# A decoder layer whose gate/up products use seven block products on two more k tiles: eight of ten groups instead of six, with sums, a row norm and transposes at other places

## The chip, the cores and the metric

The kernel runs on one core of a Trainium2 chip. The metric is the device time of one execution in microseconds; the median of several runs is compared. The engines are named as in the profile: PE is the matrix engine and PEld its weight loads, DVE the vector engine, ACT the scalar engine, POOL the general engine, SP the engine that here only issues transfers.

## The reference

One decoder layer on 256 tokens with model width 2048, all in float32: a half-step SwiGLU network of width 5632, a token mixer, and a second SwiGLU network, each followed by a layer norm.

```
def _swiglu(x, w_gate, w_up, w_down):
    return (jax.nn.silu(x @ w_gate) * (x @ w_up)) @ w_down

h = _layer_norm(ALPHA * h + 0.5 * _swiglu(h, ffn1...), ln1_g, ln1_b)
mix = _mixer(h, ...)      # latent attention of 8 heads beside differential attention of 4 heads
h = _layer_norm(ALPHA * h + mix, ln2_g, ln2_b)
h = _layer_norm(ALPHA * h + 0.5 * _swiglu(h, ffn2...), ln3_g, ln3_b)
```

In the mixer one projection gives c_q, c_kv, a rotary key, the differential branch's queries, keys and values, and two gates. The rows of c_q and c_kv pass an RMS norm before the projections to heads. Each differential head's output rows (width 256) pass an RMS norm with gain `subg`; both branches are projected, gated by sigmoids, added and projected again.

## The kernel before

**Precision.** Each float32 weight block of 128 x 1024 (two k tiles of 512 columns) is split into a high and a low part: `split` (L154, L155) casts on ACT to a rounded format, and DVE subtracts to get the low part. A product is then three matmuls of 512 columns (`triple`, L208 to L210): high by high, high by low, low by high. The second of them, L209, is the first that reads the low part of the weights.

**The queue.** All products go through one software queue in program order. `unit(load, prep, now)` issues a unit's loads at once; `prep` (sums and split) runs when more than three units are loaded and `now` (the matmuls) when more than four are prepared. The split parts lie in a ring of six pairs (`wring`). Each `now` is one tick, and `later(n, f)` runs `f` n ticks on. A scheduler may then move instructions of an engine against each other by small distances, unless `issue_after` orders them; `behind_split(n)` puts an instruction behind the low part of the n-th last split.

**Gate/up groups.** Each of the two networks has 11 groups p=0 to 10 of two 512-column weight chunks, each chunk half gate and half up. p=0 is done plainly; p=1 to 10 run in `Hybrid.group`. There the 256 tokens and the two chunks make a 2 x 2 block product, done with seven products (forms 1, 5, 6, 7, 2, 4, 3) instead of eight for k tiles 0 to 7: each form has two weight tiles, s=0 and s=1, of two k tiles each. The remaining k tiles are done plainly, one unit of two k tiles for one chunk (letters `p` and `q` in the order strings). A *wide* group takes k tiles 8 and 9 by the same forms too: a third weight tile s=2 of 128 x 512 columns, in buffers `eraw`, with its token side in `Extra`. A group that is not wide is called *narrow* here. The weight sides of forms 5, 6 and 4 are sums of two blocks, added in place on DVE (L426) ahead of the split; the sum for form 7 comes by an accumulating transfer that POOL issues (L428).

```
order = "15pp6p72q4q3q"        # wide
order = "15pp6p7p2q4q3qq"      # narrow, from p=2 on
hy.group(..., p % 3 != 1, p > 1)   # wide for p = 2, 3, 5, 6, 8, 9
```

The results go by `sum_done` (sums with an earlier copy, L882) to `half` (the product with silu of the gate, L866) and, transposed by `turn_out` (L712), to DRAM. The rows come back as `hraw`, and 13 and 16 ticks after p=10 begins to be queued `split_h` splits two of these row blocks for the down projection (`h`), among the splits of p=9 and p=10. The mixer's two gates use `Hybrid` too, with `small=True`.

**Mixer.** `c_norm(b, i)` computes the RMS norm of a half's c_q or c_kv rows (its last step, the product with the gain, is L1125) and two ticks later transposes them by `turn_out`. `ckv2_done` calls it for c_kv as soon as the last columns are there. `diff_head(h)` has four steps, scores, `turn` (transposes of the probabilities, L1100), `values` (with the norm of the output rows `orow`, L1258) and `turn2` (transposes of these, L1265, and their split `od`); step i of head h runs 2 + 6h + 3i ticks on, beside the products of a gate group.

Of the kernel before, what the change touches and what calls it, by code (L numbers as in the profile page):

```python
# [15 lines left out]
ALU = mybir.AluOpType  # L16
# [7 lines left out]
KF = DFF // P  # L24
# [35 lines left out]
def layer_kernel(ctx: ExitStack, tc: tile.TileContext, a: dict, out: bass.AP):  # L60
    nc = tc.nc
    V, S, GP, PE = nc.vector, nc.scalar, nc.gpsimd, nc.tensor
# [4 lines left out]
    small = ctx.enter_context(tc.tile_pool(name="small", bufs=1))  # L67
# [35 lines left out]
    def later(n, fn):  # L103
        uid[0] += 1
        heapq.heappush(todo, (step[0] + n, uid[0], fn))
# [47 lines left out]
    def split(hi, lo, src):  # L153
        cast[0] = S.copy(hi, src)  # L154
        lows[0] = V.tensor_tensor(out=lo, in0=src, in1=hi.bitcast(F32), op=ALU.subtract)  # L155
        return lows[0]
# [37 lines left out]
    def unit(load, prep, now, later_on=None):  # L194
        if load is not None:
            load()
        loaded.append((prep, now, later_on))
        advance(*ahead)

    def next_pair():  # L200
        assert len(ring) > len(prepared) + lag[0], (len(ring), len(prepared), lag[0])
        catch_up(len(ring) - 1)
        pair = ring.pop(0)
        ring.append(pair)
        return pair

    def triple(o, xh, xl, wh, wl, first, last, again=False):
        PE.matmul(o, xh, wh, start=first, stop=False, skip_group_check=again)  # L208
        PE.matmul(o, xh, wl, start=False, stop=False, skip_group_check=again)  # L209
        PE.matmul(o, xl, wh, start=False, stop=last, skip_group_check=again)  # L210
# [133 lines left out]
    def behind_split(n):  # L344
        return tc.issue_after(line[-n].ins) if len(line) >= n else nullcontext()

    def split_in_line(strict, *a):
        with behind_split(1) if strict else nullcontext():
            line.append(split(*a))

    class Hybrid:
# [22 lines left out]
        def group(self, w0, w1, done, wide=False, seeded=False, gates=False):  # L374
            banks = {}
            small = self.small
            n2, n3, q5, n1 = [t[:, i, :] for t in self.snaps for i in range(2)]
            R = self.raws
# [12 lines left out]
            def bank(n):  # L391
                first = n not in banks
                if first:
                    banks[n] = mm_bank()
                return banks[n], first
# [7 lines left out]
            end_s = 2 if wide else 1  # L403

            def source(name, s):
                w, j0 = blocks[name]
                if s < 2:
                    return w[j0 + s]
                i = j0 // 2
                return w[4][:, i * 512:(i + 1) * 512]  # L410

            def seventh(p, s):
                load_block, src, add, b = plan[p]
                st = {}
                tiles = G if s < 2 else 1

                def load():
                    if s < 2 and load_block in there:
                        return
                    nc.sync.dma_start(R[load_block][s], source(load_block, s))  # L420

                def prep():
                    t = R[src][s]
                    if add is not None and (small or p != 7):
                        with nullcontext() if small else behind_split(s + 1):
                            V.tensor_tensor(out=t, in0=t, in1=R[add[1]][s], op=ALU.add)  # L426
                    if not small and p == 6:
                        nc.gpsimd.dma_start(R["12"][s], source("22", s), accum_op=ALU.add)  # L428
                    pair = [v[:, :tiles * 512] for v in next_pair()]
                    split_in_line(not small, *pair, t)  # L430
                    st["pair"] = [v.rearrange("p (g n) -> p g n", g=tiles) for v in pair]

                def now():
                    o, first = bank(b)
                    wh, wl = st["pair"]
                    for g in range(tiles):
                        if s < 2:
                            xh, xl = (v[:, 2 * s + g, :] for v in self.seven.at_[p])
                        else:
                            xh, xl = self.extra.at_[p]  # L440
                        triple(o, xh, xl, wh[:, g, :], wl[:, g, :], first and g == 0,
                               s == end_s and g == tiles - 1 and p in stops, b in "XZ" or seeded)
                    if s == end_s and p in after:
                        after[p]()
                unit(load if load_block else None, prep, now)
# [403 lines left out]
    def ffn(n, x, wgu, wdn, residual, g, bt, each, first=None, between=None, nxt=None, cols=None, norm=None, pending=None):  # L849
# [78 lines left out]
        for p in range(1, KF // 4):  # L928
            if p == KF // 4 - 1:
                for i, q in enumerate((3, 4, 0)):  # L930
                    later(3 + 3 * i, lambda q=q: get_h(q))
                later(13, lambda: split_h(3))
                later(16, lambda: split_h(4))
            hy.group(wgu[2 * p], wgu[2 * p + 1],
                     lambda n, b, bank, snap, op, p=p: sum_done(2 * p + n, b, bank, snap, op),
                     p % 3 != 1, p > 1)
        ln = LayerNorm(0.5, residual, g, bt, each, nxt, cols,
                       ((24, 26, 48, 50) if pending is None else (13, 14, 60, 62), (94, 97, 100, 103)),
                       35 if cols is None else None, pending, () if pending is None else (17, 32, 67, 82))
# [10 lines left out]
        for p in range(2):  # L950
# [30 lines left out]
            else:  # L981
                call(len(units) - 8, widen)
            down.run(wdn[2 * p], wdn[2 * p + 1], units, forms,
                     lambda m, b, bank, sign, p=p: ln.fold(2 * p + m, b, bank, sign),
                     lambda m, b, bank, p=p: ln.evac(2 * p + m, b, bank), calls, 8 * p)
# [119 lines left out]
    def mixer(x):  # L1105
# [11 lines left out]
        def c_norm(b, i):  # L1117
            c = c_row[b][:, i * RANK:(i + 1) * RANK]
            junk = tmp_tile([P, RANK], "junk")
            ss = sm(1, "ss")  # L1120
            S.activation(junk, c, AF.Square, accum_out=ss)
            ms = sm(1, "ms")
            V.tensor_scalar(out=ms, in0=ss, scalar1=1.0 / RANK, scalar2=None, op0=ALU.mult)
            r = rstd(ms, RMS_EPS, 1)
            V.scalar_tensor_tensor(out=c, in0=c, scalar=r, in1=gain[:, i * RANK:(i + 1) * RANK],  # L1125
                                   op0=ALU.mult, op1=ALU.mult)
            turns[i, b] = dram.tile([P, 512], F32, name=nm("turn"))
            later(2, lambda: turn_out(c, turns[i, b]))
# [7 lines left out]

        def ckv2_done(b, bank):
            S.copy(c_row[b][:, 768:1024], bank[:, 0:256])
            c_norm(b, 1)
            kr = kr_row[b]  # L1140
            V.memset(kr, 0.0)
            rope(kr[:, 0:32].unsqueeze(1), kr[:, 64:96].unsqueeze(1), bank[:, 256:320], b, 1)
            V.tensor_copy(kr[:, 160:256].rearrange("p (a c) -> p a c", a=3)[:, 0:3:2],
                          kr[:, 0:96].rearrange("p (a c) -> p a c", a=3)[:, 0:3:2])
            later(7, lambda: to_cols(kr, krT, b, 2))
# [124 lines left out]

        for h in range(DH):
            for i, f in enumerate(diff_head(h)):
                later(2 + 6 * h + 3 * i, f)
        gate(1, 2, c_back)
        qT = [cols_proj(a["wuq"][c], cn, 4, "qT") for c in range(2)]
        qrT = act_tile([P, 4, T], F32, "qrT")
# [217 lines left out]
```

## Time and profile before

| | |
|---|---|
| median of 3 runs | 1975.17 us (1974.82 to 1975.22) |
| profiled execution | 1975.91 us |
| span of the profiled execution | 1973.9 us, 25650 instructions |
| clock granted to PE | 0.998 of full |
| PE / PEld busy | 1959.4 / 1622.2 us |
| DVE / ACT / POOL busy | 1759.6 / 1260.5 / 287.3 us |
| bytes moved | 484.64 MB, mean 246 GB/s |

The span is what the trace covers; the execution's time has 2.0 us around it. A timeline row gives start, duration, engine, source line, operation, output and inputs; in brackets stands how long the engine was idle before it and who ended that. A row of waits gives the engine and what it waited for, the total in us, how often, and the longest. In the groups by line, the numbers after the bar are busy us, mean ns of one, and idle us before. A matmul is pipelined, so its duration is longer than the step from one to the next.

### The profile page before, as it was taken

What the parts mean: (1) busy time and instruction counts of PE and PEld (TensorE: products, weight loads), DVE (VectorE), ACT (ScalarE), POOL (GpSimd) and SP (SyncE); (2) the same over time, 40 slices, a digit from 0 to 9 for tenths busy, and PEclk for the clock granted to TensorE, in tenths of its full rate; (3) what the DMA queues carried; (4) which work ended last, traced back from release to release, by engine and by line L of the source; (5) the groups of instructions that cost most, each with busy time, mean ns of one, the idle gap of its engine ahead of it and who ended that gap; (6) DMA issues with size and microseconds to landing.
All of it is one profiled execution on the core that took longest, in us unless ns stands there. A gap on an engine that the chain in (4) does not pass through costs nothing.

```text
span 1973.9 us, 25650 instructions
## 1 busy us (share of the span) xinstructions
PE 1959.4 (99%) x8796; PEld 1622.2 (82%) x8796; DVE 1759.6 (89%) x2143; ACT 1260.5 (64%) x1630; POOL 287.3 (15%) x499
## 2 busy tenths in 40 slices
PE   9999999999999999999999999999999999999997
PEld 8888878888888898888887888888888888888886
DVE  8899999999898879988977677789999999999986
ACT  6666666766656566666667765556676766665661
POOL 0112211122100011002223120001212111210000
PEclk9999999999999999999999999999999999999999
DMA  8978888778776667667667668578888877786763
GB/s 318 284 219 270 276 265 249 223 221 297 279 231 227 210 218 257 236 223 259 223 203 243 232 210 275 199 261 256 247 283 279 248 239 237 238 323 234 274 232 123
DMA packets 145747, 484.64 MB, mean 246 GB/s; under 512 B 20768, under 2 KB 20816, under 8 KB 145616
## 3 DMA queue, kind: packets, MB, share of 16 engines
q1 hardware_dynamic: 116208, 397.99, 57.8%
q0 software_dynamic: 29408, 85.02, 16.2%
q8 instruction: 69, 1.13, 0.2%
q14 instruction: 62, 0.51, 0.1%
HBM read 454.08 MB, written 28.84 MB: 245 GB/s over the span
## 4 chain that ended last, share of the span: by engine, by line
PE 94%; DVE 2%; DMA 1%; ACT 1%; issue 1%; SPq 0%; POOL 0%; DVEq 0%; ACTq 0%; POOLq 0%
PE mm L209 30%; PE mm L210 30%; PE mm L208 30%; PE tr L210 1%; PE tr L209 1%; PE tr L208 1%; DVE wring L155 1%; ACT wring L154 1%; PE tr L668 0%; DMA sraw<-in_wgm_dram 0%; DVE sraw L426 0%; DMA sraw<-in_gu_dram 0%; DMA turn<-blocks 0%; PE tr L1298 0%; PE tr L1300 0%
## 5 line engine op out<-in xcount | busy, mean ns | idle before, releaser
L154 ACT CAST wring<-raw 128x1024 fp32r<-128x1024 f32 (+2 forms) x475 | 491.0, 1037 | 319.0 <-PE mm L210 229.9
L155 DVE TENSOR_TENSOR wring<-raw,wring 128x1024 fp32r<-128x1024 f32 (+2 forms) x475 | 566.5, 1200 | 101.4 <-ACT wring L154 99.5
L154 ACT CAST wring<-sraw 128x1024 fp32r<-128x1024 f32 x436 | 452.6, 1052 | 220.0 <-DVE sraw L426 99.9
L155 DVE TENSOR_TENSOR wring<-sraw,wring 128x1024 fp32r<-128x1024 f32 x436 | 520.9, 1217 | 29.3 <-ACT wring L154 25.5
L209 PE MATMUL mm<-wring,h 128*128 128x512 f32 (+2 forms) x1260 | 485.1, 385 | 0.1
L210 PE MATMUL mm<-wring,h 128*128 128x512 f32 (+2 forms) x1260 | 485.2, 385 | 0.0
L208 PE MATMUL mm<-wring,h 128*128 128x512 f32 (+2 forms) x1260 | 484.8, 385 | 0.0
L209 PE MATMUL mm<-wring,xs 128*128 128x512 f32 x776 | 302.3, 390 | 0.0
L208 PE MATMUL mm<-wring,xs 128*128 128x512 f32 x776 | 302.2, 389 | 0.0
L210 PE MATMUL mm<-wring,xs 128*128 128x512 f32 x776 | 302.0, 389 | 0.0
L209 PEld LDWEIGHTS mm<-wring,h 128*128 128x128 f32 x1260 | 236.7, 188 | 48.6 <-DVE wring L155 2.1
L208 PEld LDWEIGHTS mm<-wring,h 128*128 128x128 f32 x1260 | 236.7, 188 | 47.0 <-ACT h L154 0.6
L210 PEld LDWEIGHTS mm<-wring,h 128*128 128x128 f32 x1260 | 236.7, 188 | 46.9 <-DVE h L155 0.7
L426 DVE TENSOR_TENSOR sraw<-sraw,sraw 128x1024 f32<-128x1024 f32 x168 | 198.4, 1214 | 3.7 <-DMA sraw<-in_wdv_dram 1.6
L209 PEld LDWEIGHTS mm<-wring,xs 128*128 128x128 f32 x776 | 145.7, 188 | 31.2 <-DVE wring L155 0.8
L210 PEld LDWEIGHTS mm<-wring,xs 128*128 128x128 f32 x776 | 145.7, 188 | 30.0
L208 PEld LDWEIGHTS mm<-wring,xs 128*128 128x128 f32 x776 | 145.6, 188 | 30.0
L714 POOL DMA_DIRECT2D hT<-blocks x176 | 97.0, 563 | 393.0 <-DVE blocks L712 392.9
L209 PE MATMUL mm<-wring,x 128*128 128x512 f32 x348 | 135.8, 390 | 0.6 <-DVE wring L155 0.6
L208 PE MATMUL mm<-wring,x 128*128 128x512 f32 x348 | 135.5, 390 | 0.0
L210 PE MATMUL mm<-wring,x 128*128 128x512 f32 x348 | 135.3, 389 | 0.0
L428 POOL DMA_DIRECT2D sraw<-in_gu_dram x40 | 35.5, 888 | 340.7 <-DVE sraw L426 337.2
(307 smaller groups left out, 2205.7 us busy)
## 6 DMA issues: line engine op xcount, KB each, us to landing
raw<-in_gu_dram SPq DMA_DIRECT2D x167, 512.0 KB, 4.5
sraw<-in_gu_dram SPq DMA_DIRECT2D x160, 512.0 KB, 5.4
raw<-in_dn_dram SPq DMA_DIRECT2D x140, 512.0 KB, 4.9
sraw<-in_gu_dram POOLq DMA_DIRECT2D x40, 512.0 KB, 6.7
sraw<-in_dn_dram SPq DMA_DIRECT2D x36, 512.0 KB, 5.6
hraw<-hT POOLq DMA_DIRECT2D x68, 256.0 KB, 5.9
raw<-in_w_out_dram SPq DMA_DIRECT2D x32, 512.0 KB, 4.5
eraw<-in_gu_dram SPq DMA_DIRECT2D x48, 256.0 KB, 5.9
```

The source lines that it names most:

```text
L154: cast[0] = S.copy(hi, src)
L155: lows[0] = V.tensor_tensor(out=lo, in0=src, in1=hi.bitcast(F32), op=ALU.subtract)
L208: PE.matmul(o, xh, wh, start=first, stop=False, skip_group_check=again)
L209: PE.matmul(o, xh, wl, start=False, stop=False, skip_group_check=again)
L210: PE.matmul(o, xl, wh, start=False, stop=last, skip_group_check=again)
L426: V.tensor_tensor(out=t, in0=t, in1=R[add[1]][s], op=ALU.add)
L428: nc.gpsimd.dma_start(R["12"][s], source("22", s), accum_op=ALU.add)
L714: nc.gpsimd.dma_start(to.rearrange("(g r) (i f) -> i r g f", g=4, i=4)[i], t[32 * i:32 * (i + 1), :].rearrange("r (g f) -> r g f", g=4))
```

## The change

1. Groups p=2 to 9 are wide, eight of ten, where p=2, 3, 5, 6, 8 and 9 were. It holds in both networks.
2. In `prep` of forms with a DVE sum, the sums for s=1 and s=2 are both issued with the tile s=1, and the split's DVE part is ordered behind the last of them. In the groups with `small` nothing is ordered.
3. The row norm of c_kv (`c_norm(b, 1)`) runs 28 ticks later for the first half and 35 for the second, instead of at once.
4. The fourth step of each differential head, the transposes of its rows, runs one tick later.

```
-                    if add is not None and (small or p != 7):
-                        with nullcontext() if small else behind_split(s + 1):
-                            V.tensor_tensor(out=t, in0=t, in1=R[add[1]][s], op=ALU.add)
+                    last = None
+                    if add is not None and (small or p != 7):
+                        for i in {0: (0,), 1: tuple(range(1, end_s + 1)), 2: ()}[s]:
+                            with nullcontext() if small else behind_split(s + 1):
+                                last = V.tensor_tensor(out=R[src][i], in0=R[src][i], in1=R[add[1]][i], op=ALU.add)
...
-                    split_in_line(not small, *pair, t)
+                    with tc.issue_after(last.ins) if last is not None and not small else nullcontext():
+                        split_in_line(not small, *pair, t)
...
-                     p % 3 != 1, p > 1)
+                     1 < p < KF // 4 - 1, p > 1)
...
-            c_norm(b, 1)
+            later(28 + 7 * b, lambda: c_norm(b, 1))
...
-                later(2 + 6 * h + 3 * i, f)
+                later(2 + 6 * h + 3 * i + i // 3, f)
```

Three lines come in ahead of L426, so that the sum is L428 in the changed kernel, and all later lines move by three.

DVE around form 5 of group p=3 of the first network; `sraw_460`, `sraw_461` and `eraw_468` are its sums for s=0, 1 and 2, and `raw` blocks are plain ones. Before:

```order
L155 TENSOR_TENSOR wring_105<-sraw_460,wring_104 128x1024
L882 TENSOR_TENSOR gus_1097<-mm_801,snap_471 128x512
L866 TENSOR_TENSOR hb_990<-gus_1093,sg_1095 128x256
L155 TENSOR_TENSOR wring_103<-sraw_461,wring_102 128x1024
L866 TENSOR_TENSOR hb_1035<-gus_1097,sg_1099 128x256
L426 TENSOR_TENSOR eraw_468<-eraw_468 128x512
L155 TENSOR_TENSOR wring_121<-eraw_468,wring_120 128x512
```

The same place in the changed kernel:

```order
L155 TENSOR_TENSOR wring_105<-sraw_460,wring_104 128x1024
L885 TENSOR_TENSOR gus_1097<-mm_802,snap_471 128x512
L869 TENSOR_TENSOR hb_990<-gus_1093,sg_1095 128x256
L428 TENSOR_TENSOR eraw_468<-eraw_468 128x512
L155 TENSOR_TENSOR wring_103<-sraw_461,wring_102 128x1024
L869 TENSOR_TENSOR hb_1035<-gus_1097,sg_1099 128x256
L155 TENSOR_TENSOR wring_121<-eraw_468,wring_120 128x512
```

The 512-column sum stands two rows earlier, ahead of the split for s=1; all other rows keep their order.

PE where head 2's rows are transposed (`orow`), between matmuls of a gate group. Before:

```order
L208 MATMUL mm_8540<-wring_120,h_617_5431 128x512
L209 MATMUL mm_8540<-wring_121,h_617_5431 128x512
L1265 MATMUL tr_8513<-ident,orow_8412 128x128 x4
L210 MATMUL mm_8540<-wring_120,h_618_5432 128x512
L208 MATMUL mm_8540<-wring_120,h_617_5431 128x512
```

In the changed kernel:

```order
L209 MATMUL mm_8521<-wring_114,h_580_5316 128x512
L1103 MATMUL tr_8535<-ident,p_8447 128x128
L1268 MATMUL tr_8560<-ident,orow_8434 128x128 x3
L1103 MATMUL tr_8535<-ident,p_8447 128x128 x2
L1268 MATMUL tr_8560<-ident,orow_8434 128x128
L210 MATMUL mm_8521<-wring_114,h_581_5317 128x512
```

The four transposes stand some 45 matmuls later, mixed with those of the next head's probabilities (`p`).

DVE where the c_kv rows of the first half were normed, before (`c_row_5317` with its gain, then its transpose):

```order
L155 TENSOR_TENSOR wring_105<-sraw_5917,wring_104 128x1024
L706 SCALAR_TENSOR_TENSOR f_5897<-t_5895,y_5893 128x1
L155 TENSOR_TENSOR wring_103<-raw_5936,wring_102 128x1024
L1125 SCALAR_TENSOR_TENSOR c_row_5317<-c_row_5317,f_5897,gain_5321 128x512
L1123 TENSOR_SCALAR ms_5965<-ss_5963 128x1
L1141 MEMSET kr_row_5320 128x256
L687 TENSOR_SCALAR ve_5967<-ms_5965 128x1
L1068 TENSOR_TENSOR ropec_5982<-mm_5775,sincos 128x64
L1069 TENSOR_TENSOR ropes_5983<-mm_5775,sincos 128x64
L712 STREAM_TRANSPOSE blocks_5989<-c_row_5317 128x512
```

Where the same rows (`c_row_5339`) stand in the changed kernel, in the second gate group:

```order
L428 TENSOR_TENSOR sraw_5919<-sraw_5919,sraw_5925 128x1024
L709 SCALAR_TENSOR_TENSOR f_6321<-t_6319,y_6317 128x1
L155 TENSOR_TENSOR wring_119<-raw_6295,wring_118 128x1024
L1128 SCALAR_TENSOR_TENSOR c_row_5339<-c_row_5339,f_6321,gain_5343 128x512
L155 TENSOR_TENSOR wring_117<-sraw_5925,wring_116 128x1024
L715 STREAM_TRANSPOSE blocks_6351<-c_row_5339 128x512
L155 TENSOR_TENSOR wring_115<-sraw_5926,wring_114 128x1024
```

The norm's steps now stand between splits and sums of that group; the rope steps of `kr_row` stay where they were.

## Prediction

> **What bounds the kernel now.** I read the page's busy times and chain first, then TensorE's waits, then the two engines' timelines inside the gate/up groups, because that is where the change acts. The page, its busy times and its chain that ended last:
>
> ```profile
> PE 1959.4 (99%) x8796; PEld 1622.2 (82%) x8796; DVE 1759.6 (89%) x2143; ACT 1260.5 (64%) x1630; POOL 287.3 (15%) x499
> PE 94%; DVE 2%; DMA 1%; ACT 1%; issue 1%; SPq 0%; POOL 0%; DVEq 0%; ACTq 0%; POOLq 0%
> ```
>
> TensorE is the bound: 99% busy and 94% of the chain. A busy PE could still be slow, so I take its pace from the timeline; these two are the first and last of thirteen matmuls that follow each other in group p=3:
>
> ```profile
> 141.05 0.39 PE L210 MATMUL mm<-wring,x 128*128 128x512 f32 x1
> 143.77 0.39 PE L210 MATMUL mm<-wring,x 128*128 128x512 f32 x1
> ```
>
> Twelve steps in 2.72 us: a 512-column matmul costs 0.227 us, whatever its 0.39 us of pipelined length says. There are two ways to get faster: fewer matmuls, or fewer moments in which PE has nothing to take. The second way is small. The waits of PE's weight loads, over the whole span and then in the windows 745 to 760, 255 to 262 (two rows), 136 to 175, 379 to 385, 1410 to 1420, 1535 to 1540 and 1654 to 1660 us:
>
> ```profile
> PEld mm L209 <- DVE wring L155: 5.5, 14, 0.8
> PEld tr L1265 <- DVE orow L1258: 1.9, 1, 1.9
> ...
> PEld mm L209 <- DVE wring L155: 1.3, 4, 0.5
> ...
> PEld mm L209 <- DVE wring L155: 1.5, 3, 0.6
> PEld mm L208 <- ACT wring L154: 0.6, 1, 0.6
> ...
> PEld mm L209 <- DVE wring L155: 0.2, 1, 0.2
> ...
> PEld mm L209 <- DVE wring L155: 0.4, 1, 0.4
> ...
> PEld mm L209 <- DVE wring L155: 0.2, 1, 0.2
> ...
> PEld mm L209 <- DVE wring L155: 0.3, 1, 0.3
> ...
> PEld mm L209 <- DVE wring L155: 0.4, 1, 0.4
> ```
>
> So all waits for a split's low part come to 5.5 us, and I can place most of them. VectorE stands close behind PE. Busy times of the stretches of wide group p=2, of narrow group p=4 (with the first three matmuls of p=5) and of the second mixer gate group; the columns are PE, PEld, DVE, ACT, POOL, clock, DMA share, GB/s:
>
> ```profile
> 95.20:135.30 40.10, 40.10 (x179) 33.20 (x177) 38.43 (x45) 26.78 (x35) 6.18 (x10) 1.00 0.78 244
> 174.80:216.30 41.50, 41.50 (x185) 34.35 (x183) 39.98 (x43) 27.20 (x33) 8.15 (x13) 1.00 0.89 271
> 782.50:823.30 40.80, 40.80 (x182) 33.78 (x181) 40.01 (x38) 25.57 (x28) 2.17 (x4) 1.00 0.63 227
> ```
>
> The clock is full. DVE's 96% is not its need, because durations of neighbours overlap in the records. What it needs shows in starts. DVE's timeline around form 5 of p=3, with the splits ahead of form 1 of p=3 and of p=4 (first and last row) and the first matmuls that read those two splits:
>
> ```profile
> 125.86 2.35 DVE L155 TENSOR_TENSOR wring<-sraw,wring 128x1024 fp32r<-128x1024 f32 x2
> ...
> 131.00 0.68 DVE L882 TENSOR_TENSOR gus<-mm,snap 128x512 f32<-128x512 f32 x1
> 131.60 1.21 DVE L155 TENSOR_TENSOR wring<-sraw,wring 128x1024 fp32r<-128x1024 f32 x1
> 132.74 0.68 DVE L882 TENSOR_TENSOR gus<-mm,snap 128x512 f32<-128x512 f32 x1
> 133.34 0.41 DVE L866 TENSOR_TENSOR hb<-gus,sg 128x256 f32<-128x256 f32 x1
> 133.67 1.22 DVE L155 TENSOR_TENSOR wring<-sraw,wring 128x1024 fp32r<-128x1024 f32 x1
> 134.81 0.42 DVE L866 TENSOR_TENSOR hb<-gus,sg 128x256 f32<-128x256 f32 x1
> 135.14 0.68 DVE L426 TENSOR_TENSOR eraw<-eraw 128x512 f32<-128x512 f32 x1
> 136.74 0.69 DVE L155 TENSOR_TENSOR wring<-eraw,wring 128x512 fp32r<-128x512 f32 x1 [0.92 <-ACT wring L154]
> 137.35 2.35 DVE L155 TENSOR_TENSOR wring<-raw,wring 128x1024 fp32r<-128x1024 f32 x2
> 139.62 2.35 DVE L426 TENSOR_TENSOR sraw<-sraw,sraw 128x1024 f32<-128x1024 f32 x2
> ...
> 167.25 2.35 DVE L155 TENSOR_TENSOR wring<-sraw,wring 128x1024 fp32r<-128x1024 f32 x2
> ```
>
> ```profile
> 131.90 0.39 PE L209 MATMUL mm<-wring,xs 128*128 128x512 f32 x1
> 138.70 0.43 PE L209 MATMUL mm<-wring,x 128*128 128x512 f32 x1
> 172.10 0.39 PE L209 MATMUL mm<-wring,xs 128*128 128x512 f32 x1
> ```
>
> From start to start a 1024-column operation takes 1.135 us (137.35 to 139.62 is two), a 512-column one 0.60 (131.00 to 131.60), a 256-column one 0.33 (133.34 to 133.67). The first split of the pair at 125.86 is ready at 125.86 + 1.22 = 127.08 and is read at 131.90: a lead of 4.8 us. One wide group later it is 172.10 − (167.25 + 1.22) = 3.6. That group thus cost DVE 1.2 us of lead, and inside it the lead had fallen to 138.70 − (137.35 + 1.21) = 0.14, as good as nothing. Of the 1.2, one row explains 0.92: DVE waits at 136.74, because the sum over the 512-column block at 135.14 comes right ahead of the split that needs ScalarE's cast of it.
>
> **Part 1, groups p=4 and p=7 of both layers become wide.** A narrow group is 7 forms × 4 tiles × 3 + 8 plain × 12 = 180 matmuls. A wide one is 7 × 5 × 3 + 6 × 12 = 177. Four groups change, so 12 matmuls go: **−2.72 us**, on PE's path throughout.
>
> The price is DVE. A wide group has 20 splits and 6 sums of 1024 columns, 7 splits, 3 sums, 3 gate/up sums and 2 transposes of 512, and 4 products of 256: 26 × 1.135 + 15 × 0.60 + 4 × 0.33 = 39.8 us, against PE's 177 × 0.2267 = 40.1. A narrow one has two more of the 1024 kind, and ten fewer of the 512 kind: 36.1 against 40.8. The old sequence wide, wide, narrow gave 4.7 us back every third group; the new one has eight wide groups in a row. By this count DVE still keeps up, by 0.3 a group, provided that it never waits. That hangs on part 2.
>
> [...] I count by starts.
>
> **Part 2, the order of the sums.** The sum at 135.14 moves two rows forward, ahead of the split at 133.67; ScalarE can cast while DVE splits. The 0.92 us wait goes, and a wide group then costs at most the other 0.3 of lead. What is late next: nothing in rows, if the cast takes place in those 1.1 us. The stalls that such groups show today (0.2, 0.4, 0.2, 0.3, 0.4 in five windows, 1.5 of weight load) should shrink. A load overlaps the matmul ahead of it, so PE loses only part; I take half, **−0.8**; bounds 0 and −1.5.
>
> The last group's h splits, which stand in the wide group before it and today fill such a wait, now cost their own time there:
>
> ```profile
> 379.59 1.28 DVE L155 TENSOR_TENSOR h<-hraw,h 128x512 fp32r<-128x512 f32 x2
> ```
>
> That is 1.2 us of lead, once in each layer. It is covered if the lead is a good 1 us by then.
>
> **The late block.** The 1.5 + 0.6 us of waits at 255 to 262 follow a late weight block:
>
> ```profile
> 247.09 1.05 ACT L154 CAST wring<-sraw 128x1024 fp32r<-128x1024 f32 x1 [2.57 <-DMA sraw<-in_gu_dram]
> ```
>
> The second layer's same group shows only the 0.3 at 1535 to 1540, so this is a matter of one transfer, perhaps of this one execution. With more lead it is absorbed: **−1.5** (bounds 0 and −2.1). Wide groups replace two 512 KB blocks by four of 256 KB, so the bytes stay the same.
>
> **Part 3, the row norm.** Two norms stood among the splits at 739 to 755 us:
>
> ```profile
> L1125 DVE SCALAR_TENSOR_TENSOR c_row<-c_row,f,gain 128x512 f32<-128x512 f32 x2 | 1.5, 740 | 0.0
> L712 DVE STREAM_TRANSPOSE blocks<-c_row 128x512 f32<-128x512 f32 x2 | 1.4, 698 | 0.0
> ```
>
> These 2.9 us and some one-column steps cause the 1.3 us of waits at 745 to 760. I take **−1.1** (bounds 0 and −1.3). They land among the splits of the second gate group (782 to 823 us), where DVE is 98% busy by the records, but has idle time around:
>
> ```profile
> 777.67 1.23 DVE L155 TENSOR_TENSOR wring<-sraw,wring 128x1024 fp32r<-128x1024 f32 x1 [1.19 <-ACT wring L154]
> 811.04 2.36 DVE L155 TENSOR_TENSOR wring<-raw,wring 128x1024 fp32r<-128x1024 f32 x2 [0.71 <-ACT wring L154]
> ```
>
> A DVE that waits for ScalarE's cast, which waits for PE to free a buffer, is a DVE with a full lead: 1.9 us are to spare. If the cover is missing there, the same 1.1 comes back. The transposes' DMAs on POOL's queue move too; POOL is busy 2.17 of 40.8 us there, and the normed rows are read only by projections after the attention heads.
>
> **Part 4, the diff rows' transposes one step later.** One of four heads has PE waiting 1.9 us of weight load for its rows; on PE itself:
>
> ```profile
> PE tr L1265 <- DVE orow L1258: 1.4, 1, 1.4
> ```
>
> The new place is some 45 matmuls later, 10 us, among the next head's transposes. The wait goes: **−1.4** (bounds −1.9 and, if the transposes' bank is then taken a little late, by the smallest wait above, +0.2). What could be late next is the split of the transposed rows, but its readers come after the heads.
>
> **Sum.** For small waits at new places in the wide groups I add **+0.5** (two of 0.25, about the size of the five above; bounds 0 and, for each of the five once more, 1.5). −2.72 − 0.8 − 1.5 − 1.1 − 1.4 + 0.5 = −7.0 us. The profiled execution took 1975.91 us (1973.9 of span and 2.0 around it): 1968.9. From the median, 1975.17, the whole sum gives 1968.2, and 1969.7 without the late block. I forecast **1968.9**.
>
> **Rivals.** *DVE falls short by a little.* If an operation takes 0.02 to 0.03 us longer than counted, a wide group is about 40.4 us and loses 0.35. The lead of 0.14 + 0.92 = 1.06 in p=3 is gone after three more groups, and six groups cost 6 × 0.35 − 1.06 = 1.0 per layer: 1971.0. For it: the margin of 0.3 is 0.7% of my count. Against: the count takes in every row. 0.18.
>
> *A moved wait returns.* Row norm or transposes stall at the new place, +1.1 to 1.4: 1970.3. For it: DVE has 40.01 of 40.8 there. Against: the idle rows. 0.12.
>
> *The wait is not cured, and the kernel gets slower.* Should ScalarE still cast the block late, every wide group after the second costs 1.2 us with no narrow group to give it back. Six groups × 1.2 = 7.2 per layer, 14.4 in all; of the gains 2.72 + 1.1 + 1.4 = 5.2 stay: 1975.9 + 9.2 = 1985. It decides from 5.2 / 12 = 0.43 us per group. For it: the narrow groups' 4.7 us, gone for good. Against: the sum is placed ahead of a 1.1 us split. 0.07.
>
> *Late blocks without slack.* A wait like that 2.57 us, once in each of several groups that have little lead, +1.5 four times: 1975. For it: DMA share 0.89 in one stretch. Against: one such row in two layers. 0.07.
>
> *Full durations count:* 26 × 1.22 + 15 × 0.68 + 4 × 0.42 = 43.6 us a wide group, 3.5 over PE. Four new ones cost 14: 1983. [...] Against: twelve wide groups run at PE's pace now with 5.5 us of waits in the whole span. 0.02. Another 0.02 for what I do not see.
>
> **How the numbers follow.** The forecast has 0.52, its own range 1967.5 to 1970.5. The range takes in the first two rivals as well (0.82). Its bottom is the sum with every stall at its larger bound: 0.7 + 0.6 + 0.2 + 0.5 below, and 0.5 for new waits that do not come, 1966.4. Its top is the median less the matmuls alone, plus those 0.5: 1973.0. About what a measurement of this kernel can tell from no change is 0.2%, 3.95 us, so faster means below 1971.22: the forecast, most of the second rival and half of the first, 0.71. Same, 0.17: the rest of these and most of the late blocks. Slower, 0.12: not cured, full durations, the unseen, some late blocks.
>
> **What would show it.** Right: 8784 matmul records; around form 5 of each wide group no DVE wait near 0.9 us; a lead at form 1 that falls by less than 0.4 per wide group; no waits at 745 to 760, nor of the diff transposes for their rows. Wrong: waits for a split's low part that grow from group p=5 on, or a DVE that runs through wide groups without idle time while PE waits; then the count of 39.8 is too low. Rows of a wait for the norm's place at 780 to 825 would refute part 3, a wait of readers of the transposed rows part 4.

## The result, and the profile after

The changed kernel takes 1973.1 us in the median of 22 runs (1971.03 to 1975.41), the kernel before 1975.37 us in as many runs beside it (1973.57 to 1979.37). The ratio is 0.9987 with a 95% interval of 0.9981 to 0.9993, that is 1.4 to 3.8 us faster. The forecast was 6.3 us under the earlier median; the sign was right, but the gain is about a third of the one forecast. The forecast's range ended at 1973.0: the time as it stands is 0.1 above that, and 2.27 us off the earlier median of 1975.17, from which that end was worked out, give 1972.9. By the prediction's own line for faster, 1971.22, the time is no more than the same. The profiled execution took 1972.85 us, its span is 1971.1 against 1973.9.

The page's busy times and its chain of the changed kernel:

```profile
PE 1955.1 (99%) x8784; PEld 1620.0 (82%) x8784; DVE 1773.5 (90%) x2175; ACT 1265.5 (64%) x1650; POOL 291.0 (15%) x503
PE 95%; DVE 2%; DMA 1%; issue 1%; ACT 0%; SPq 0%; DVEq 0%; ACTq 0%
```

Twelve matmuls are gone, as counted, which is 2.72 us. That is nearly all of the 2.8 us by which the spans differ: on balance the waits saved nothing. The largest waits of PE's weight loads over the span show that they are other waits now:

```profile
PEld mm L209 <- DVE wring L155: 4.5, 9, 1.1
PEld tr L1248 <- ACT pt L1105: 1.6, 1, 1.6
...
PEld mm L208 <- ACT wring L154: 1.2, 1, 1.2
```

The wait for the diff rows (1.9 us before) has left the head of the list; in its place stands one of 1.6 us for `pt`, the copy of a head's probabilities, which was 0.2 us before.

To compare stages I summed, for every matmul, the time from its start to the next start above its usual step (0.227 us at 512 columns), and call that a stall. Before and after, in us: gate/up groups of the first network 2.0 and 1.1, of the second 0.6 and 0.8; the mixer up to the heads 1.1 and 0.4; the start of the kernel 3.6 and 4.5; everything together 22.1 and 22.0. The start is the same code in both, and ranges from 3.6 to 5.0 over the profiles of this study.

Inside the wide groups the new order does what was forecast. DVE's timeline of the changed kernel around form 5 of p=3, with the pairs of splits ahead of form 1 of p=3, 4 and 5 (the rows at 126.75, 166.88 and 207.14) and the only two rows between 134 and 207 us before which DVE was idle (153.58 and 193.70):

```profile
126.75 2.37 DVE L155 TENSOR_TENSOR wring<-sraw,wring 128x1024 fp32r<-128x1024 f32 x2
...
134.56 0.70 DVE L428 TENSOR_TENSOR eraw<-eraw 128x512 f32<-128x512 f32 x1
135.16 1.24 DVE L155 TENSOR_TENSOR wring<-sraw,wring 128x1024 fp32r<-128x1024 f32 x1
136.29 0.44 DVE L869 TENSOR_TENSOR hb<-gus,sg 128x256 f32<-128x256 f32 x1
136.63 0.70 DVE L155 TENSOR_TENSOR wring<-eraw,wring 128x512 fp32r<-128x512 f32 x1
137.23 2.37 DVE L155 TENSOR_TENSOR wring<-raw,wring 128x1024 fp32r<-128x1024 f32 x2
...
153.58 1.23 DVE L155 TENSOR_TENSOR wring<-raw,wring 128x1024 fp32r<-128x1024 f32 x1 [0.17 <-ACT wring L154]
...
166.88 2.36 DVE L155 TENSOR_TENSOR wring<-sraw,wring 128x1024 fp32r<-128x1024 f32 x2
...
193.70 1.23 DVE L155 TENSOR_TENSOR wring<-raw,wring 128x1024 fp32r<-128x1024 f32 x1 [0.17 <-ACT wring L154]
...
207.14 2.35 DVE L155 TENSOR_TENSOR wring<-sraw,wring 128x1024 fp32r<-128x1024 f32 x2
```

The sum at 134.56 is ahead of the split now, and the idle 0.92 us are gone. The first matmuls that read the first split of each of those three pairs:

```profile
132.80 0.39 PE L209 MATMUL mm<-wring,xs 128*128 128x512 f32 x1
...
172.92 0.39 PE L209 MATMUL mm<-wring,xs 128*128 128x512 f32 x1
...
213.04 0.39 PE L209 MATMUL mm<-wring,xs 128*128 128x512 f32 x1
```

With 1.23 us for a split the leads are 4.82, 4.81 and 4.67 us. A wide group now costs DVE 0.0 to 0.15 us of lead, where it cost 1.2 before. The count by starts, 39.8 us of DVE against 40.1 of PE, nearly holds: from pair to pair it is 40.13 and 40.26 us, of which DVE is idle for 0.17, so a group's work took it 40.0 and 40.1 us. The rival in which full durations count would have each group lose 3.5 us; the lead that stands still from p=3 to p=5 decides against it.

But one wait in these groups stayed, and came to the second network as well. ACT's timeline at the change from p=5 to p=6 of both networks:

```profile
247.38 1.05 ACT L154 CAST wring<-sraw 128x1024 fp32r<-128x1024 f32 x1 [2.71 <-DMA sraw<-in_gu_dram]
...
1521.17 1.05 ACT L154 CAST wring<-sraw 128x1024 fp32r<-128x1024 f32 x1 [2.51 <-DMA sraw<-in_gu_dram]
```

### The profile page after: what moved, and what is told of

Same layout as the page of the kernel before. It is cut to its first block, busy times and chain, and to the rows that moved or that the text cites. A ratio compares the mean times of both kernels' runs of the same rounds, so it can differ in the third digit from the quotient of the medians.

```text
span 1971.1 us, 25747 instructions
## 1 busy us (share of the span) xinstructions
PE 1955.1 (99%) x8784; PEld 1620.0 (82%) x8784; DVE 1773.5 (90%) x2175; ACT 1265.5 (64%) x1650; POOL 291.0 (15%) x503
## 4 chain that ended last, share of the span: by engine, by line
PE 95%; DVE 2%; DMA 1%; issue 1%; ACT 0%; SPq 0%; DVEq 0%; ACTq 0%
PE mm L209 30%; PE mm L210 30%; PE mm L208 30%; DVE wring L155 1%; PE tr L208 1%; PE tr L210 1%; PE tr L209 1%; DMA sraw<-in_gu_dram 1%; PE tr L671 0%; DVE sraw L428 0%; ACT wring L154 0%; DMA raw<-in_gu_dram 0%; PE tr L1228 0%; PE tr L1301 0%; PE tr L1303 0%
## 5 line engine op out<-in xcount | busy, mean ns | idle before, releaser
L154 ACT CAST wring<-raw 128x1024 fp32r<-128x1024 f32 (+2 forms) x467 | 482.2, 1038 | 296.5 <-PE mm L210 207.2
L155 DVE TENSOR_TENSOR wring<-raw,wring 128x1024 fp32r<-128x1024 f32 (+2 forms) x467 | 559.1, 1206 | 95.4 <-ACT wring L154 92.8
L210 PE MATMUL mm<-wring,h 128*128 128x512 f32 (+2 forms) x1248 | 480.2, 385 | 0.0
L208 PE MATMUL mm<-wring,h 128*128 128x512 f32 (+2 forms) x1248 | 480.2, 385 | 0.0
L209 PE MATMUL mm<-wring,h 128*128 128x512 f32 (+2 forms) x1248 | 479.8, 385 | 0.0
L428 DVE TENSOR_TENSOR sraw<-sraw,sraw 128x1024 f32<-128x1024 f32 x168 | 200.2, 1229 | 3.5 <-DMA sraw<-in_wdv_dram 1.6
L208 PE MATMUL mm<-wring,x 128*128 128x512 f32 x336 | 130.8, 390 | 0.8 <-ACT wring L154 0.8
L209 PE MATMUL mm<-wring,x 128*128 128x512 f32 x336 | 131.0, 390 | 0.5 <-DVE wring L155 0.5
L210 PE MATMUL mm<-wring,x 128*128 128x512 f32 x336 | 130.6, 389 | 0.0
```

The costliest lines, as they stand in the source:

```text
L428: last = V.tensor_tensor(out=R[src][i], in0=R[src][i], in1=R[add[1]][i], op=ALU.add)
```

## The experiments

All times are against the kernel before on the same chip in the same session, since its median alone ranges from 1974.42 to 1975.37 us over the sessions; the changed kernel itself was measured in the first session alone, so other kernels are compared with it by their ratios to the kernel before. A profile shows one execution: those of experiments 1 and 9 were 2.8 and 4.4 us above their kernels' medians, those of 5 and 8 3.3 and 2.4 us below, so stalls read from them need not add up to the differences of the medians.

**1. Six wide groups, the rest as changed.**

```
-                     1 < p < KF // 4 - 1, p > 1)
+                     p % 3 != 1, p > 1)
```

> The changed kernel with the old choice of wide groups (six of ten), all else as changed. Theory A (matmuls are worth their 0.227 us, DVE keeps up): 12 matmuls come back, so it is 2.7 us slower than the changed kernel and 1 to 1.5 us faster than the kernel before, from the row norm's wait (1.0) and the waits of the wide groups (0.5). Theory B (the new wide groups cost DVE or transfers about what they save): the same as the changed kernel within 1 us, 2.5 us faster than before.

Measured: 1974.36 us beside 1974.42, ratio 0.9999 (0.9990 to 1.0007). By the ratios this is 2.4 us slower than the changed kernel, close to theory A's 2.7. Theory A's 1 to 1.5 us faster than before did not show in the median, though the interval (2.0 us faster to 1.4 slower) does not exclude it; theory B's 2.5 it does. In the profile the gate/up groups of both networks run without any stall (0.0 us), against 1.9 us in the changed kernel. That is not the price of the wide groups alone, since ACT's late block was late by only 1.6 and 0.4 us here, against 2.7 and 2.5. The profile also has a wait in the mixer that is 0.3 us in the changed kernel; whether the faster executions have it is not known:

```profile
PEld tr L1228 <- ACT dkT L737: 3.3, 1, 3.3
```

**2. Eight wide groups, each sum ahead of its own split, as before.**

```
-                        for i in {0: (0,), 1: tuple(range(1, end_s + 1)), 2: ()}[s]:
-                            with nullcontext() if small else behind_split(s + 1):
-                                last = V.tensor_tensor(out=R[src][i], in0=R[src][i], in1=R[add[1]][i], op=ALU.add)
+                        with nullcontext() if small else behind_split(s + 1):
+                            V.tensor_tensor(out=t, in0=t, in1=R[add[1]][s], op=ALU.add)
...
-                    with tc.issue_after(last.ins) if last is not None and not small else nullcontext():
-                        split_in_line(not small, *pair, t)
+                    split_in_line(not small, *pair, t)
```

> The changed kernel with eight wide groups but the sums issued as before, each ahead of its own split. Theory A (a wide group then loses 0.92 to 1.2 us of lead, and no narrow group gives it back): waits for the low part of a split in every wide group from p=4 on, 5 to 7 us in each network, so 10 to 14 us slower than the changed kernel, about 8 to 12 slower than before. Theory B (ACT and the queue have enough room, the order of the sums does nothing): within 1 us of the changed kernel.

Measured: 2002.58 us beside 1974.42, ratio 1.0141 (1.0127 to 1.0154). Theory A holds, at more than twice its price: 28 us slower than the kernel before, where it said 8 to 12. DVE's waits at form 5 of p=3 and p=4, and the waits of PE's weight loads over the span:

```profile
137.00 0.69 DVE L155 TENSOR_TENSOR wring<-eraw,wring 128x512 fp32r<-128x512 f32 x1 [0.87 <-ACT wring L154]
...
178.18 0.69 DVE L155 TENSOR_TENSOR wring<-eraw,wring 128x512 fp32r<-128x512 f32 x1 [0.69 <-ACT wring L154]
```

```profile
PEld mm L209 <- DVE wring L155: 26.4, 49, 1.5
PEld mm L208 <- ACT wring L154: 8.8, 16, 0.7
```

The stalls in the groups are 11.9 and 12.7 us, and 5.8 us more follow in the first down projection, most of it at one place near 593 us. Without the new order the eight wide groups would have made the kernel slower: the two edits only work together.

**3. The row norm at once, as before.**

```
-            later(28 + 7 * b, lambda: c_norm(b, 1))
+            c_norm(b, 1)
```

> The changed kernel with the row norm of c_kv done at once, as before. Theory A (its DVE steps stood among tight splits): waits for the low part of about 1.3 us of weight load come back at 740 to 760 us, 1.0 us slower than the changed kernel. Theory B (the wait is only paid elsewhere): no wait there or another wait gone, within 0.3 us.

Measured: 1974.28 us beside 1974.42, ratio 0.9998 (0.9989 to 1.0006). The waits of PE's weight loads from 740 to 762 us are back, to the digit:

```profile
PEld mm L209 <- DVE wring L155: 1.3, 4, 0.5
```

In the changed kernel no weight load waits for anything between 740 and 830 us, so nothing shows at the new place either. The stalls of the mixer up to the heads are 1.1 us here and 0.4 there. Theory A holds, with 0.7 us by the stalls. The ratios put it 2.2 us above the changed kernel, with intervals that overlap.

**4. The diff rows' transposes at their old step.**

```
-                later(2 + 6 * h + 3 * i + i // 3, f)
+                later(2 + 6 * h + 3 * i, f)
```

> The changed kernel with the transposes of the diff rows at their old step. Theory A (the wait only moved from these rows to the copy of the next head's probabilities on ACT): the wait of 1.4 to 1.9 us for the rows comes back near 1065 us, the one of 1.1 to 1.6 us for the copied probabilities near 1077 us goes, and the time stays within 0.5 us of the changed kernel. Theory B (the step is worth its 1.4 us): 1.4 us slower.

Measured: 1970.68 us beside 1974.42, ratio 0.9979 (0.9969 to 0.9988). That is the lowest median of the study, and it makes part 4 of the change a loss, which neither theory had. The time alone does not separate it from the changed kernel, since the intervals overlap; the traces help. From the first score matmul of the differential heads to the last value matmul of the other ones PE has the same work in all these kernels. The two ends in the kernel before, the changed kernel and this one:

```profile
948.16 0.38 PE L1225 MATMUL tr<-dkT,dqT 128*128 128x128 f32 x2
...
1150.44 0.38 PE L1315 MATMUL tr<-pt,v 128*128 128x128 f32 x2
```

```profile
945.87 0.49 PE L1228 MATMUL tr<-dkT,dqT 128*128 128x128 f32 x2
...
1148.67 0.38 PE L1318 MATMUL tr<-pt,v 128*128 128x128 f32 x2
```

```profile
944.27 0.38 PE L1228 MATMUL tr<-dkT,dqT 128*128 128x128 f32 x2
...
1145.41 0.38 PE L1318 MATMUL tr<-pt,v 128*128 128x128 f32 x2
```

That is 202.3, 202.8 and 201.1 us. By the same measure the six other profiles with the new step (experiments 1, 2, 3, 5, 8 and 12) have 202.6 to 205.1 us, and the five others with the old one (6, 7, 9, 10 and 11) 200.5 to 201.9. The two sets do not overlap, but these kernels differ in more than the step. The pairs that differ in the step alone say 1.7 us (the changed kernel and this one) and 0.7 (12 and 9); 8 and 6, which differ in the edit of experiment 5 too, say 1.2. The medians of the same pairs differ by 1.6, 0.8 and 2.0 us, the new step always being the slower. So it costs some 1 to 2 us. The wait for `pt` is down to 0.2 us, as in theory A, and the wait for the rows is there again, at 0.8 us:

```profile
PEld tr L1268 <- DVE orow L1261: 0.8, 1, 0.8
```

**5. The changed kernel, with the kT copies asked for one tick earlier.**

```
-        kT = [cols_proj(a["wuk"][c], cn, 4, "kT", 4, 8) for c in range(2)]
+        kT = [cols_proj(a["wuk"][c], cn, 4, "kT", 4, 7) for c in range(2)]
```

In the changed kernel the wait for `pt` looks like one of ACT's order. ACT's timeline of the changed kernel, and the matmul that waited:

```profile
1076.22 0.62 ACT L737 COPY kT<-turned 128x512 f32<-128x512 f32 x1 [1.13 <-DMA turned<-turn]
1076.75 1.04 ACT L154 CAST wring<-raw 128x1024 fp32r<-128x1024 f32 x1
1077.69 0.47 ACT L1105 COPY pt<-tr 128x384 f32<-128x384 f32 x1
```

```profile
1078.22 0.70 PE L1248 MATMUL tr<-dv,pt 128*128 128x256 f32 x2 [1.14 <-ACT pt L1105]
```

> The changed kernel in which the copies of the turned keys (kT) to columns are asked for one tick earlier in the program; on ACT the copy of head 3's probabilities (pt) then stands ahead of the last kT copy and of one weight cast instead of behind them. Theory A (the 1.1 to 2.4 us wait of head 3's values comes from ACT's order, where pt is queued behind a kT copy that waits for its transfer): the wait for pt falls by about 1.5 us and the time by 1 to 2 us against the changed kernel. Theory B (PE is only ahead of the whole attention chain by then, so the time is lost at the next step anyway): the wait shows at another place of the heads and the time is the changed kernel's within 0.5 us.

Measured: 1975.2 us beside 1974.98, ratio 1.0001 (0.9993 to 1.0010). By the ratios this is 2.8 us above the changed kernel, not within theory B's 0.5; the intervals just touch, and single executions range from 1971.87, the profiled one, to 1977.94. About the wait theory B is right: the one for `pt` is gone, and the transposes of the same head's probabilities wait instead:

```profile
PEld tr L1103 <- DVE p L1237: 3.0, 1, 3.0
```

**6. The kernel of experiment 4, with the product rows read back later.** In the changed kernel POOL issues the reading back of the first product rows, six transfers of 256 KB, at 196 and 198 us (two) and from 237 to 239 us (four), long before DVE makes their low parts, the first at 384. Here it is held behind the last accumulating transfer ahead of p=10.

```
+                        summed[0] = nc.gpsimd.dma_start(R["12"][s], source("22", s), accum_op=ALU.add)
...
+                with tc.issue_after(summed[0].ins):
+                    nc.gpsimd.dma_start(raw[:, b, :], hT[q, b])
```

> The kernel with the transposes of the diff rows at their old step, and in it the reading back of the first product rows (hraw), which POOL issues in the groups p=5 and p=6, held behind the last accumulating transfer ahead of p=10. Theory A (these 1.5 MB meet the burst of weight blocks at the change of group and make the first block of p=6 late): ACT's wait of 2.5 to 2.7 us for a weight block near 247 and 1521 us goes, and with it 1.7 to 2.3 us of PE's waits in the gate/up groups; about 1968.5 us. Theory B (the burst alone makes the block late): the waits stay and the time is that of the kernel without this edit, 1970.7.

Measured: 1978.78 us beside 1974.98, ratio 1.0014 (1.0005 to 1.0024). Both times are missed: the cause is shown, the cure failed. No cast waits for a block near 247 or 1521 us any more, in this or in any other kernel in which the rows are read back later (7, 8, 9, 10, 11 and 12), while in all the others, the one before included, ACT waited 1.6 to 2.9 us near 247. The transfers of that block, which were issued at 239.08 in the changed kernel and at 239.47 here, say it directly; the last number is the time from issue to landing in us:

```profile
sraw<-in_gu_dram SPq DMA_DIRECT2D x1, 512.0 KB, 8.2
```

```profile
sraw<-in_gu_dram SPq DMA_DIRECT2D x1, 512.0 KB, 4.9
```

With four of the row transfers (1 MB) issued just before it the block took 3.3 us longer. But the casts of the first rows on ACT moved too: at 237.2 and 242.9 us in the changed kernel, they now stand right behind the reading, and ACT is idle until it lands:

```profile
383.90 0.62 ACT L154 CAST h<-hraw 128x512 fp32r<-128x512 f32 x1 [5.29 <-DMA hraw<-hT]
```

**7. Experiment 6 with p=10 wide as well** (`p > 1` as the condition).

> The kernel of the run above with the last group, p=10, wide as well. Theory A (a wide group costs DVE no lead): 6 matmuls less, 1.36 us faster than the run above. Theory B (the splits of the first product rows, 2.4 us of DVE beside p=9 and p=10, need the narrow group's slack): waits for the low part of splits in p=10, 0.5 to 2 us in each network, so the same or slower.

Measured: 1984.14 us beside 1974.98, ratio 1.0044 (1.0031 to 1.0056), 5.4 us above experiment 6. The waits are of theory B's kind, but the largest part lies behind p=10: 4.9 us of stalls near 586 us in the first down projection, where experiment 6 has none.

**8. The changed kernel with the edits of experiments 5 and 6.**

> The changed kernel, its transposes of the diff rows at the new step, with both edits: the kT copies asked for one tick earlier and the product rows read back later. Theory A: 1.7 to 2.3 us from the late block and 1 to 2 us from the wait for pt, so 3 to 4 us faster than the changed kernel, about 1969, and the stalls between 1062 and 1090 us below those of the kernel with the old step (2.8 us). Theory B (the later step of the transposes is worth nothing even without that wait): the same time as the kernel with the old step and the rows read back later, within 0.5 us.

Measured: 1980.75 us beside 1974.98, ratio 1.0029 (1.0018 to 1.0041). It has both disturbances and cures neither; it tells nothing beyond 5 and 6.

**9. As experiment 6, but behind the transfers of p=8** (`summed` keeps all of them, and the fourth last is taken).

> The kernel with the transposes of the diff rows at their old step, and the reading back of the first product rows (hraw) held one group less long than before: behind the accumulating transfers of p=8, in the stretch of the group where few weight blocks are under way, 40 us ahead of their split. Theory A (those 1.5 MB make the block of p=6 late, and nothing else is wrong with eight wide groups): no ACT wait for a block near 247 and 1521 us, none for hraw near 385 us, stalls in the gate/up groups of both networks below 0.3 us; 1968.4 us, 2.3 below the kernel without this edit. Theory B (wherever they are read they push some block late): a wait of 1.5 to 3 us for a block at another group; 1970 to 1972.

Measured: 1977.07 us beside 1974.52, ratio 1.0016 (1.0008 to 1.0025). The late block is gone as in theory A, but neither theory's time came. The casts of the rows have again come along with the reading, 40 us earlier than meant:

```profile
345.08 0.62 ACT L154 CAST h<-hraw 128x512 fp32r<-128x512 f32 x1 [6.43 <-DMA hraw<-hT]
```

Stalls in the groups are 5.4 us in each network. Reading these rows at a quiet place with their casts held well behind it has not been tried.

**10. Experiment 9 with p=10 wide as well.**

> The run above with the last group, p=10, wide as well. Theory A (a wide group costs DVE no lead, so the splits of the product rows still find 2.4 us): 6 matmuls less, 1.36 us faster than the run above. Theory B (DVE has about 1 us of lead there and the row splits take 2.4): waits for the low part of splits of 0.5 to 1.5 us in p=9 and p=10 of each network, and the gain of 1.36 is lost.

Measured: 1980.73 us beside 1974.52, ratio 1.0027 (1.0016 to 1.0039). The 1.36 us are not gained; the first down projection stalls for 6.6 us between 550 and 600 us. Why it does so behind a wide p=10 stays open.

**11. Experiment 9 with six wide groups.**

> The run before last with six wide groups instead of eight. Theory A (with the late block gone the two more wide groups per network are worth their matmuls alone): 12 matmuls more, 2.7 us slower than with eight, no stalls in the gate/up groups in either. Theory B (the wide groups have another price): a difference under 1.5 us, with stalls among the groups p=4 to 9 of the kernel with eight.

Measured: 1972.19 us beside 1974.52, ratio 0.9991 (0.9982 to 0.9999). Fewer wide groups are faster here, by 4.9 us, against both theories. The groups run without a stall, but the rows also come less late: POOL issues their reading at 333.2 us here and at 337.2 in experiment 9, and ACT waits for them 1.9 us instead of 6.4. So this pair does not say how much of the 4.9 us is slack of the narrow groups.

**12. The changed kernel with the edit of experiment 9.**

> The changed kernel as it is, transposes at the new step, with the product rows read back beside p=8. Theory A: the late block is worth 1.5 to 2 us here too, so about 1971.3, and the new step of the transposes costs 2 to 3 us against the old one, with a wait of 1 to 2.5 us for the copied probabilities near 1076 us. Theory B (the new step costs nothing by itself, the runs only scattered): within 1 us of the kernel with the old step.

Measured: 1977.89 us beside 1974.52, ratio 1.0017 (1.0008 to 1.0027). The first half of theory A fails as in experiment 9; against that kernel the time is 0.8 us more, within theory B's bound. The heads take 202.6 us against 201.9, and the wait for `pt` is there as in the changed kernel (1.6 us).

## Why the prediction was right and wrong

The time came out at the upper end of the range, which stood for the matmuls alone plus 0.5 us, and that is what happened. Of the 4.3 us that the forecast expected from waits on balance, the two profiles show 0.1, or 1.0 without the later start of the second. The outcome "same" had a chance of 0.17, "faster" 0.71.

Part 1 was right in its terms: 12 matmuls of 0.227 us, and a DVE that needs a little less than PE by starts. The margin is only about 0.1 us and not 0.3, but the lead stands still, and the first rival, a DVE short by 0.35 us a group, did not come.

Part 2 was right, and weightier than its term of 0.8 us says. It was costed as the end of small waits, while its real worth is that it makes part 1 possible: without it the kernel takes 2002.6 us. The third rival's mechanism is confirmed by experiment 2, but its price, 14.4 us before gains, was too low: experiment 2 is 28 us slower than the kernel before, where that rival had 9 after the gains. Six groups × 1.2 us took a late split as delaying only itself. ACT's casts then come late as well (8.8 us of waits over the span), and the stalls go on into the first down projection.

The late block's −1.5 was a wrong step. I took it for one transfer's accident, from the one execution in which the second network did not have it, and held that it would be absorbed. It has a cause, the product rows whose reading meets the weight blocks at the change to p=6 (8.2 us to landing beside them, 4.9 without). ACT's wait is in the first network of every kernel that reads them there, and more lead did absorb a part: in the four profiles with eight wide groups (the changed kernel, 3, 4 and 5) a wait of ACT of 1.7 us cost nothing, and waits of 1.9 to 3.2 us cost 0.3 to 2.0, while 2.57 us cost 1.7 in the kernel before. Whether six wide groups in the new order would hide more is not shown, because in experiment 1 the waits were only 1.6 and 0.4 us. What the traces do show is that DVE, with no narrow group behind the late block, has no idle time at all in p=6 to 8 of the changed kernel, whereas the narrow p=7 of experiment 1 has 1.4 us of it. This is the fourth rival's mechanism, in one block of each network instead of four in all and at 0.8 to 1.1 us each instead of 1.5; I had given it 0.07. All told, the waits in the groups fell by 0.7 us, where my terms for them (−0.8, −1.5 and +0.5) said 1.8.

Part 3 was right: −1.1 forecast, 0.7 in stalls and the 1.3 us of weight-load waits back to the digit when it is undone. At the new place nothing waits for it.

Part 4 was the largest error, −1.4 forecast. The heads take 0.5 us longer than before, and 1 to 2 us longer than without this part. The step that failed is "the wait goes": I looked for what would be late next among the readers of the transposed rows, and it was the next head's own chain. The wait for the rows was one place at which PE met an attention chain that runs over ACT, DVE and POOL's transfers. With that wait gone, PE came earlier to the next place, and waited there for `pt`; with `pt` moved forward, it waited for `p` (experiment 5). The second rival, with a chance of 0.12, came nearest; it took 1.1 to 1.4 us where 1.9 were lost, and it looked for the wait at the transposes' own new place. Two things stay open. One is why the chain itself is later with the new step, which makes the step a loss and not merely no gain. The head's norm on ACT, for instance, begins at 1060.80 us in the changed kernel and at 1057.35 in experiment 4:

```profile
1060.80 0.37 ACT L1254 ACTIVATE junk<-tr 128x256 f32<-128x256 f32 x1
```

```profile
1057.35 0.41 ACT L1254 ACTIVATE junk<-tr 128x256 f32<-128x256 f32 x1
```

That is 3.5 us later, while PE is only 1.6 us later at the start of the heads; orders on ACT and POOL differ in several places, and I have not separated them. The other is why the heads of experiment 4 are 1.1 us shorter than before with the transposes at the same step.

So of −7.0 us: −2.72 came, about −0.7 of −1.1 came, −0.7 of −1.8 came, and +0.5 came where −1.4 was meant. This makes −3.6; the two profiles differ by 2.8 us, with 0.9 us more at the start of this execution, and the medians by 2.3.

## What to carry to other kernels

When a bubble is closed that lets a producer keep pace with a full consumer, count the producer by starts and check the lead from group to group: a lead that stands still is the proof. What goes with the old arrangement is the idle time in which the producer could catch up, here 1.4 us in a narrow group and none in three wide ones, so find out what each late transfer then costs. A wait that sits in a chain through several engines is worth only what the next place of that chain leaves; follow the whole chain to its slowest engine before booking it as a gain. And a late transfer that shows once may have a cause: look at what else is in flight at that moment before calling it chance.

## What the runs showed of the hardware

After some stalls PE came back at half speed for a while; in experiment 9 the granted clock was 0.50 from 350.52 to 353.93 us. Matmuls of experiment 9 after 2.52 and 0.76 us of idle time:

```profile
348.65 0.51 PE L208 MATMUL mm<-wring,xs 128*128 128x512 f32 x1 [2.52 <-ACT wring L154]
349.91 0.50 PE L209 MATMUL mm<-wring,xs 128*128 128x512 f32 x1 [0.76 <-DVE wring L155]
...
351.28 0.63 PE L210 MATMUL mm<-wring,xs 128*128 128x512 f32 x1
351.70 0.63 PE L208 MATMUL mm<-wring,xs 128*128 128x512 f32 x1
...
353.84 0.44 PE L210 MATMUL mm<-wring,xs 128*128 128x512 f32 x1
```

From 350.47 to 353.84 us, 3.4 us, a matmul takes 0.43 us instead of 0.227, which costs 1.6 us on top of the stall; the stall sums above contain it.

The length of the idle time alone did not decide whether this came. Experiment 9 around the stall above and experiment 1 around an idle time of 2.9 us, two stretches of 3.41 us each; behind the length of the stretch stands PE's busy time, and the granted clock is the third number from the right:

```profile
347.11:350.52 3.41, 1.12 (x4) 0.71 (x5) 1.23 (x2) 3.41 (x6) 0.00 (x0) 1.00 0.23 93
350.52:353.93 3.41, 3.41 (x10) 2.60 (x9) 3.41 (x4) 2.90 (x4) 0.00 (x0) 0.50 0.01 2
```

```profile
944.10:947.51 3.41, 2.15 (x10) 1.45 (x8) 3.41 (x5) 0.00 (x1) 1.41 (x3) 1.00 0.22 56
947.51:950.92 3.41, 1.79 (x9) 1.53 (x10) 3.41 (x5) 2.99 (x4) 1.43 (x4) 1.00 0.61 154
```

In experiment 9 PE was idle for 2.3 us of the first stretch, and the second ran at half clock. In experiment 1 PE was idle for 1.3 and 1.6 us, and both stretches ran at full clock. In experiment 3 PE was idle for 2.21 us up to 1078.54 us, in experiment 6 for 2.7 us between 1660 and 1664, in experiment 7 for 2.2 us between 384 and 388; the 4 us from 1078, 1664 and 388 us on had a mean granted clock of 0.57, 0.57 and 0.58, as 3.4 us at half clock and the rest at full would give. After 1.4 us near 1066 us in the kernel before and 1.1 us near 1078 us in the changed kernel the clock stayed full (1.00 up to 1071.47 and 1083.75 us). What decides beside the length is not shown.
